# Unread matrix products by bank and by need, a norm's root on VectorE, and new charges in the planner of a four-layer hybrid kernel

## The chip, the cores and the metric

The kernel runs on one core of a Trainium2 chip. The metric is the device time of one launch in microseconds (us). In the notation of the profile, PE is TensorE's matrix products, PEld its weight loads, DVE is VectorE, ACT is ScalarE, POOL is GpSimd and SP is SyncE, which here only issues transfers.

## The reference

A token matrix `x` of 512 x 1024 goes through four layers. Each adds a mixer of the normalised activations and then a gated feed-forward block; a last norm ends it. The four mixers are different: a recurrent one with a state per head (RWKV-7), a banded attention, a chunked gating unit, and gated linear attention. Everything is float32.

```python
def rwkv7_mix(x, ...):
    ...
    def step(state, inp):
        r_t, d_t, k_t, v_t, kk_t, a_t = inp
        sa = jnp.einsum('bhvk,bhk->bhv', state, kk_t)
        state = (state * d_t[:, :, None, :]
                 - sa[..., None] * (kk_t * a_t)[:, :, None, :]
                 + v_t[..., None] * k_t[:, :, None, :])
        return state, jnp.einsum('bhvk,bhk->bhv', state, r_t)
    ...
    mean = jnp.mean(y, -1, keepdims=True)
    var = jnp.mean(jnp.square(y - mean), -1, keepdims=True)
    y = ((y - mean) * lax.rsqrt(var + RW_GN_EPS)).reshape(B, S, D) * gn_g + gn_b
    ...

def reference(x, ...):
    h = x
    for i in range(DEPTH):
        hn = rmsnorm(h, norm_mix[i])
        m = rwkv7_mix(hn, ...) if i == 0 else swa_sink_mix(hn, ...) if i == 1 else sgu_chunk_mix(hn, ...) if i == 2 else gla_mix(hn, ...)
        h = h + m
        h = h + swiglu(rmsnorm(h, norm_ffn[i]), ffn_w_in[i], ffn_w_out[i])
    return rmsnorm(h, norm_final)
```

The part that the change edits in the computation is the norm over each head's 64 values (`mean`, `var`, the reciprocal root) behind the recurrence; there are 16 heads.

## The kernel before, in words

**Products.** A float32 weight is split into a rounded part (`whi`, cast on ACT) and the rest (`wlo`, subtracted on DVE); the activations likewise. Each product is then three matrix products that accumulate in one bank of PSUM (`mm3`). The feed-forward blocks use a seven-product scheme for 2 x 2 blocks (`seven`, `hidden`, `out_fast`), whose sums DVE takes out of the banks into `slot` and `h`. PSUM has eight banks, one tile `ps` each.

**The recurrent mixer** fills the span up to about 520 us. The projections come first. Then four groups of four heads (`n` = 0 to 3) each go through a *preparation* (`rwkv_prepare`, `rwkv_products`, `rwkv_inverse`, `rwkv_direct`) that makes, for eight blocks of 64 tokens, small triangular matrices and their inverses, and through a *chain* (`rwkv_chain`) that carries the state from block to block. `rwkv_inverse` has a row of about thirty small DVE instructions (`et<-et`) that depend on each other, and then rounds of 64 x 64 products, with their results copied or masked by ACT and DVE (`mt`, `iv`). In the chain each step goes from PE (`ps<-vu,tok`) to DVE (`st<-ps,pend`) and back to PE. After every second pair of blocks `rwkv_out` takes the head norm, transposes on PE (`ps<-ident,out`) and splits the result (`rk`); it runs eight times in all. `rwkv_out_proj` multiplies the first six of eight pieces by the output weights while the last group's norm runs, and `out_proj` the last two.

**The order.** Nothing is issued as it is written. `Program.record` keeps every instruction with its dependences, and `Program.run` then sets the order on all engines by a simulated clock: an instruction's price is `price` (line 264), the earliest candidate within a window of 700 is issued, and PSUM banks are handed out by free slots. In the program's own order, preparation and chain alternate by `ORDER = "pppppcpcpcpc"` (line 31): five pieces of the next group's preparation, then chain and preparation by turns. Each engine executes its own row in the order that the planner left, so a wrong price costs a wait on the chip.

**Unread products.** The planner also issues products of the 128 x 128 identity with itself that nobody reads; line 478 (`product`) is their only source, and each takes a bank of its own. Two rules put them in. `keep_warm` (line 397) fills a gap on PE that the planner foresees and that is at least 450 ns long, one product after the other until the next real product is due. `ahead_of_cold` (line 416) puts one ahead of a real product when the columns that went through PE in the last 3,413 ns would fall under `DENSE` = 3,550. A product is charged 224 ns, or 448 when the window before had under `BUSY` = 3,350 columns. A float32 product such as this one has two records in the trace.

**The head norm.** `rwkv_out` (line 1363) takes two sums on DVE. The mean, the variance and the root are small 128 x 8 instructions on POOL: the multiplication by 1/64 with a tile of constants, the same and an addition for the variance, and in `rsqrt8` (line 1400) one DVE instruction for the first guess and then thirteen on POOL, three rounds of four. The other norms use `rsqrt`, whose ten instructions are all on DVE.

## Time and profile before

| | us |
|---|---|
| median of 3 runs (2602.77 to 2609.27) | 2609.03 |
| the profiled execution | 2608.54 |
| span in the profile | 2606.8 |
| PE busy | 2550.0 |
| DVE busy | 1796.5 |
| ACT busy | 1317.5 |
| POOL busy | 371.2 |

The mean granted clock of PE is 0.995. Between the span and the execution's time lie 1.7 us. A row of the busy-time view by windows gives a stretch, its length, and for each engine the busy time with the number of records in brackets, then the granted clock (1.00 is full), the share of the DMA engines and their rate. A row of the timeline gives the start, the length, the engine, the line, the operation, what it writes and reads, and the number of merged records; in square brackets stands the time that the engine sat idle before it, and what ended that. Nearly every instruction carries line 234, where the recorder calls the engine; so the names of tiles tell instructions apart, and line 478 the unread products. PE's ends are modelled: the distance between two starts is the better measure there.

### The profile page before, as it was taken

To read this page: it belongs to the slowest core of one execution; us is meant where nothing else is said; L and a number is where in the kernel's file an instruction comes from. 1 tells how busy PE (TensorE), PEld (TensorE's weight loads), DVE (VectorE), ACT (ScalarE), POOL (GpSimd) and SP (SyncE) were. 2 spreads that over 40 slices of the span, in tenths; PEclk is the share of its full clock that TensorE was granted. 3 is DMA by queue.
4 is the path that set the end of the run, shared out by engine and by line. 5 is a ranking of instruction groups with operands and counts; after the bars stand their busy time and mean duration, and the time that the engine had idled before them with its cause. 6 is when DMAs were issued, how large, how long until landed. Compare 5 with 4: busy or idle time off the path is not lost.

```text
span 2606.8 us, 37773 instructions
## 1 busy us (share of the span) xinstructions
PE 2550.0 (98%) x14482; PEld 2073.6 (80%) x14482; DVE 1796.5 (69%) x2801; ACT 1317.5 (51%) x2163; POOL 371.2 (14%) x517
## 2 busy tenths in 40 slices
PE   9999999999999999999999999999999999999998
PEld 8577777998878766988787888888878777888786
DVE  7674765478778864787777555477768634577868
ACT  4534354375646445655464333465546523555545
POOL 0000111112121332121212000012111000112111
PEclk9999999999999999999999999999999999999999
DMA  4210001379898422788995322399897221489885
GB/s 168 68 60 10 10 4 58 108 180 211 225 212 192 104 89 49 159 213 220 215 234 146 97 89 85 79 213 230 206 214 183 93 81 57 95 215 225 217 196 127
DMA packets 126581, 367.32 MB, mean 141 GB/s; under 512 B 13360, under 2 KB 20016, under 8 KB 126400
## 3 DMA queue, kind: packets, MB, share of 16 engines
q0 software_dynamic: 41472, 138.43, 29.7%
q1 hardware_dynamic: 84928, 226.47, 26.8%
q8 instruction: 114, 1.87, 0.3%
q14 instruction: 67, 0.55, 0.1%
HBM read 360.39 MB, written 2.10 MB: 139 GB/s over the span
## 4 chain that ended last, share of the span: by engine, by line
PE 50%; DMA 5%; DVE 4%; issue 3%; ACT 2%; POOL 0%; SPq 0%; DVEq 0%; POOLq 0%; ACTq 0%
PE ps L234 50%; DMA wraw<-ffn_w_b 3%; DMA wraw<-ffn_o_a 2%; DVE slot L234 2%; ACT slot L234 1%; ACT whi L234 1%; DVE wlo L234 1%; DMA wraw<-ffn_w_a 1%; DVE h L234 0%; PE ps L478 0%; DVE mx L234 0%; POOL wraw L234 0%; DMA slot<-slot 0%; POOL slot L234 0%; SPq L234 0%
## 5 line engine op out<-in xcount | busy, mean ns | idle before, releaser
L234 PE MATMUL ps<-whi,slot 128*128 128x512 f32 (+1 forms) x5072 | 1556.0, 384 | 18.6 <-DVE h L234 8.2
L234 PEld LDWEIGHTS ps<-whi,slot 128*128 128x128 f32 x5072 | 941.8, 188 | 200.9 <-issue 24.1
L234 DVE TENSOR_TENSOR wlo<-wraw,whi 128x1024 fp32r<-128x1024 f32 (+2 forms) x632 | 725.9, 1154 | 402.0 <-ACT whi L234 399.1
L234 ACT CAST whi<-wraw 128x1024 fp32r<-128x1024 f32 (+3 forms) x632 | 625.5, 993 | 725.3 <-PE ps L234 551.7
L234 PE MATMUL ps<-wlo,slot 128*128 128x512 f32 (+1 forms) x2536 | 967.6, 382 | 1.3 <-DVE wlo L234 1.3
L234 PEld LDWEIGHTS ps<-wlo,slot 128*128 128x128 f32 x2536 | 476.1, 188 | 85.7 <-DVE wlo L234 5.4
L234 PE MATMUL ps<-slot,whi 128*128 128x512 f32 (+2 forms) x864 | 274.6, 396 | 0.4 <-DVE slot L234 0.3
L234 DVE TENSOR_TENSOR slot<-ps,slot 128x512 f32<-128x512 f32 (+2 forms) x287 | 154.9, 566 | 74.6 <-PE ps L234 54.3
L234 PEld LDWEIGHTS ps<-slot,whi 128*128 128x128 f32 (+2 forms) x864 | 156.8, 184 | 48.9 <-DVE slot L234 6.9
L234 POOL DMA_DIRECT2D wraw<-ffn_w_a x128 | 109.4, 855 | 513.3 <-DVE wlo L234 395.5
L234 PE MATMUL ps<-slot,wlo 128*128 128x512 f32 (+2 forms) x432 | 169.5, 393 | 0.0
L234 POOL DMA_DIRECT2D wraw<-ffn_w_b x64 | 54.8, 861 | 767.7 <-DMA wraw<-ffn_w_b 517.2
L234 DVE TENSOR_TENSOR slot<-left,slot 128x512 fp32r<-128x512 f32 (+1 forms) x214 | 137.7, 662 | 34.9 <-ACT slot L234 29.4
L234 DVE TENSOR_TENSOR h<-h,ps 128x512 f32<-128x512 f32 x192 | 127.2, 683 | 30.5 <-PE ps L234 29.0
L234 ACT CAST slot<-left 128x512 fp32r<-128x512 f32 (+1 forms) x214 | 123.9, 599 | 32.8 <-PE ps L234 26.4
L234 ACT COPY slot<-ps 128x512 f32<-128x512 f32 (+1 forms) x138 | 75.9, 564 | 57.9 <-PE ps L234 54.2
L234 PEld LDWEIGHTS ps<-slot,wlo 128*128 128x128 f32 (+2 forms) x432 | 79.5, 184 | 20.3 <-issue 3.3
L234 POOL DMA_DIRECT2D wraw<-ffn_o_a x64 | 54.7, 854 | 277.7 <-DVE wlo L234 161.0
L234 PEld LDWEIGHTS ps<-ident,slot 128*128 128x128 f32 (+2 forms) x672 | 67.8, 139 | 30.5 <-issue 7.5
L234 PE MATMUL ps<-ident,slot 128*128 128x128 f32 (+2 forms) x672 | 87.4, 265 | 2.9 <-DVE slot L234 2.1
L478 PE MATMUL ps<-ident 128*128 128x128 f32 x488 | 80.9, 302 | 4.4 <-DVE slot L234 2.2
L234 ACT COPY left<-ps 128x512 f32<-128x512 f32 x100 | 50.5, 556 | 56.9 <-PE ps L234 56.9
(279 smaller groups left out, 2301.5 us busy)
## 6 DMA issues: line engine op xcount, KB each, us to landing
wraw<-ffn_w_a SPq DMA_DIRECT2D x128, 512.0 KB, 6.4
wraw<-ffn_w_a POOLq DMA_DIRECT2D x128, 512.0 KB, 6.1
wraw<-ffn_o_a SPq DMA_DIRECT2D x64, 512.0 KB, 5.0
wraw<-ffn_o_a POOLq DMA_DIRECT2D x64, 512.0 KB, 8.1
wraw<-ffn_w_b SPq DMA_DIRECT2D x64, 384.0 KB, 3.4
wraw<-ffn_w_b POOLq DMA_DIRECT2D x64, 384.0 KB, 6.0
wraw<-ffn_o_b SPq DMA_DIRECT2D x16, 512.0 KB, 4.3
wraw<-ffn_o_b POOLq DMA_DIRECT2D x16, 512.0 KB, 8.0
```

The source lines that it names most:

```text
L234: op = self.add(eng.name, lambda: getattr(eng.target, what)(*map(real, args), **{k: real(a) for k, a in kw.items()}), *self.price(eng.name ...
L478: self.nc.tensor.target.matmul(self.ps.tile_pool.tile([P, S], F32, name="ps")[:, :P], self.ident.real(), self.ident.real(), start=True, st ...
```

## The change

1. The unread products come in batches: `products(n)` takes one bank and puts `n` products into it, where each had taken its own. `ahead_of_cold` computes how many are needed (at most four) instead of one at a time.
2. They are put in by a smaller need: `BUSY` and `DENSE` fall to 3,000 columns; `keep_warm` stops, once a count has reached `DENSE`, when the past window has over `RICH` = 4,200 columns. A product is also charged for a change of shape (`TURN`, 92 ns).
3. The head norm's mean, variance and root go from POOL to DVE: one `tensor_scalar` each for the mean and the variance and the common `rsqrt`. `rsqrt8` and the constant tiles `k8` are gone.
4. Charges: a DVE instruction that writes a state tile `st` is charged 90 ns more, one on 32 partitions 270 ns more, and no small POOL instruction less than 150 ns.

`ORDER` stays. The order on every engine follows from the new numbers. Over the whole program the unread products go from 244 to 154; PE's other 12,128 products, and their operands, are the same.

```diff
-    TICK, BUSY, DENSE = 10240 / 3, 3350.0, 3550.0
+    TICK, BUSY, DENSE, RICH = 10240 / 3, 3000.0, 3000.0, 4200.0
...
-            return 63.0 + n * (0.52 if fast else 2.1 if what == "tensor_tensor_scan" else 1.05) + 61.0 * columns, 250.0
+            slow = 90.0 if views[0].buf.name.startswith("st") else 270.0 if views[0].shape[0] == 32 else 0.0
+            return slow + 63.0 + n * (0.52 if fast else 2.1 if what == "tensor_tensor_scan" else 1.05) + 61.0 * columns, 250.0
...
-        return 37.0 + n * (0.83 if len(views) < 3 else 2.8 if views[0].dims[-1][0] < 32 else 2.4), 250.0
+        return max(150.0, 37.0 + n * (0.83 if len(views) < 3 else 2.8 if views[0].dims[-1][0] < 32 else 2.4)), 250.0
...
         while True:
-            c = 224.0 if work.get(int(t // self.TICK) - 1, 0.0) >= self.BUSY else 448.0
-            if t + c > s - self.TAIL:
-                return now
-            call()
-            self.fills += 1
+            c = 224.0 + (self.TURN if self.form[:2] != (P, P) else 0.0)
+            if work.get(int(t // self.TICK) - 1, 0.0) < self.BUSY:
+                c *= 2
+            if t + c > s - self.TAIL or self.armed and self.past(s) > self.RICH:
+                break
+            n += 1
...
-        cost = 224.0 if work.get(int(t // self.TICK) - 1, 0.0) >= self.BUSY else 448.0
-        call()
-        self.fills += 1
...
+        n = min(4, math.ceil((self.DENSE - sum_) / 280.0))
+        for _ in range(n):
+            cost = 224.0 + (self.TURN if self.form[:2] != (P, P) else 0.0)
...
-        def product():
-            self.nc.tensor.target.matmul(self.ps.tile_pool.tile([P, S], F32, name="ps")[:, :P], self.ident.real(), self.ident.real(), start=True, stop=True)
-        self.nc.warm = self.ps, product, self.nc.ops[-1]
+        def products(n):
+            t, i = self.ps.tile_pool.tile([P, S], F32, name="ps")[:, :P], self.ident.real()
+            for _ in range(n):
+                self.nc.tensor.target.matmul(t, i, i, start=True, stop=True)
+        self.nc.warm = self.ps, products, self.nc.ops[-1]
...
-        nc.gpsimd.tensor_mul(mean, mean, self.k8['mean'])
+        nc.vector.tensor_scalar(mean, mean, 1.0 / 64, None, op0=ALU.mult)
...
-        nc.gpsimd.tensor_mul(var, var, self.k8['mean'])
-        nc.gpsimd.tensor_add(var, var, self.k8['eps'])
-        self.rsqrt8(rs, var)
+        nc.vector.tensor_scalar(var, var, 1.0 / 64, 64e-5, op0=ALU.mult, op1=ALU.add)
+        self.rsqrt(rs, var)
...
-    def rsqrt8(self, y, x):
-
-        nc = self.nc
-        t = self.sm.tile([P, 8], F32, name="rs8")
-        nc.vector.tensor_scalar(y.bitcast(I32), x.bitcast(I32), -0.5, float(0x5f3759df), op0=ALU.mult, op1=ALU.add)
-        nc.gpsimd.tensor_mul(x, x, self.k8['half'])
-        for _ in range(3):
-            nc.gpsimd.tensor_mul(t, y, y)
-            nc.gpsimd.tensor_mul(t, t, x)
-            nc.gpsimd.tensor_add(t, t, self.k8['one5'])
-            nc.gpsimd.tensor_mul(y, y, t)
```

The rows of the order below are shown without their numbers; line 478 before and line 496 now are the unread products, line 234 all else.

**TensorE in the third group's inverse** (`rwkv_inverse` with the chain's products among its rounds; `mt`, `iv` and `pa` are tiles of the inverse, `vu`, `st` and `v` of the chain). Before the change the order reads:

```order
L234 MATMUL ps<-mt,pa 64x64 x3
L478 MATMUL ps<-ident 128x128
L234 MATMUL ps<-mt,pa 64x64
L478 MATMUL ps<-ident 128x128
L234 MATMUL ps<-mt,pa 64x64 x12
L234 MATMUL ps<-iv,mt 64x64 x3
L234 MATMUL ps<-vu,pr 64x64 x2
L234 MATMUL ps<-ident,out 128x128
L478 MATMUL ps<-ident 128x128
L234 MATMUL ps<-mt 64x64 x7
L478 MATMUL ps<-ident 128x128
L234 MATMUL ps<-mt 64x64
```

With the change it reads:

```order
L234 MATMUL ps<-mt,pa 64x64 x16
L234 MATMUL ps<-vu,pr 64x64 x4
L234 MATMUL ps<-v_2013,pa 64x64
L234 MATMUL ps<-qk 128x128 x2
L234 MATMUL ps<-mt 64x64 x4
L496 MATMUL ps<-ident 128x128
L234 MATMUL ps<-mt 64x64 x12
L234 MATMUL ps<-et,sel 4x512
L234 MATMUL ps<-iv,mt 64x64 x16
```

The round of sixteen `mt,pa` products stood in three pieces with an unread product between them; it now stands whole, and the next round has one unread product in it.

**TensorE in the banded attention** (the 64-row products of queries with keys, `slot`). Before the change the order reads:

```order
L234 MATMUL ps<-slot 128x256 x8
L478 MATMUL ps<-ident 128x128 x7
L234 MATMUL ps<-slot 128x128
L478 MATMUL ps<-ident 128x128 x2
L234 MATMUL ps<-slot 128x128
L234 MATMUL ps<-slot 128x256 x10
```

With the change it reads:

```order
L234 MATMUL ps<-slot 128x128 x2
L234 MATMUL ps<-slot 128x256 x8
L496 MATMUL ps<-ident 128x128 x4
L234 MATMUL ps<-slot 128x128 x2
L234 MATMUL ps<-slot 128x256 x10
```

Nine unread products in nine banks became four in one, and the second break is gone. At the second place of this kind seven became six.

**VectorE at a head norm beside an inverse** (`gvar` is the variance, `grs` the root, `et<-et` the row of the inverse, `st` the chain's state). Before the change the order reads:

```order
L234 TENSOR_SCALAR grs_2578<-gvar 128x8
L234 STREAM_TRANSPOSE et<-et 128x512
L234 TENSOR_TENSOR st_1396<-ps,pend 64x2x64
L234 TENSOR_TENSOR et<-et 128x2
L234 TENSOR_TENSOR st_1396<-ps,pend 64x2x64
L234 TENSOR_REDUCE et<-et 128x2
L234 TENSOR_TENSOR et<-et 128x8
L234 TENSOR_REDUCE et<-et 128x2x2
```

With the change it reads:

```order
L234 TENSOR_SCALAR gvar<-gvar 128x8
L234 STREAM_TRANSPOSE et<-et 128x512
L234 TENSOR_SCALAR grs_2489<-gvar 128x8
L234 TENSOR_TENSOR et<-et 128x2
L234 TENSOR_TENSOR rs_t<-grs_2489 128x8
L234 TENSOR_REDUCE et<-et 128x2
L234 SCALAR_TENSOR_TENSOR rs_t<-gvar,rs_t 128x8
L234 TENSOR_TENSOR et<-et 128x8
L234 SCALAR_TENSOR_TENSOR grs_2489<-rs_t,grs_2489 128x8
L234 TENSOR_REDUCE et<-et 128x2x2
```

The root's instructions now stand between those of the inverse, by turns, and the state's update, which stood ahead of the second of them, comes after the root.

More of the change, by code (lines that the diff above doesn't have):

```diff
@@ L433, in ahead_of_cold, with past @@
             return False
[L434 to L440 removed]
+        n = min(4, math.ceil((self.DENSE - sum_) / 280.0))
+        for _ in range(n):
+            cost = 224.0 + (self.TURN if self.form[:2] != (P, P) else 0.0)
+            if work.get(int(t // self.TICK) - 1, 0.0) < self.BUSY:
+                cost *= 2
+            self.form = P, P, 0
+            self.count(work, self.TICK, t, cost, 512.0)
+            t += cost
+        call(n)
+        self.fills += n
+        now["PE"] = t
+        return True
+    def past(self, end):
+        sum_ = 0.0
+        for b, e, c in reversed(self.recent):
+            if e <= end - self.TICK:
+                break
+            sum_ += c * (e - max(b, end - self.TICK)) / (e - b)
+        return sum_
     def count(self, work, span, t, cost, columns):
```

19 lines of the change are left out of this document (6 added, 13 removed).

## The prediction

> **What bounds the kernel now.** I read the page first, then the busy time by stretches for the whole core and for line 478 alone, then who waits for whom, then the timeline at single places. On the page:
>
> ```profile
> PE 2550.0 (98%) x14482; PEld 2073.6 (80%) x14482; DVE 1796.5 (69%) x2801; ACT 1317.5 (51%) x2163; POOL 371.2 (14%) x517
> L478 PE MATMUL ps<-ident 128*128 128x128 f32 x488 | 80.9, 302 | 4.4 <-DVE slot L234 2.2
> ```
>
> PE is busy for 98% of the span, and 488 of its records are the 244 unread products. They are 80.9 us by the profile, so what matters is where they lie, and whether PE would otherwise wait there. By stretches, the whole core in the first three rows (PE, PEld, DVE, ACT, POOL) and line 478 alone in the others (PE, PEld):
>
> ```profile
> 190.00:270.00 80.00, 78.08 (x918) 59.95 (x913) 39.39 (x81) 37.25 (x73) 6.82 (x22) 1.00 0.03 8
> 270.00:290.00 20.00, 18.35 (x212) 16.92 (x211) 19.01 (x39) 10.30 (x20) 8.27 (x21) 1.00 0.06 15
> 290.00:450.00 160.00, 154.27 (x2250) 123.59 (x2250) 106.04 (x222) 67.19 (x146) 23.09 (x72) 0.99 0.08 27
> ...
> 0.00:20.00 20.00, 17.80 (x134) 17.61 (x134) 1.00 0.90 315
> 190.00:270.00 80.00, 6.26 (x30) 4.17 (x30) 1.00 0.03 8
> 270.00:290.00 20.00, 11.27 (x98) 11.10 (x98) 1.00 0.06 15
> 290.00:450.00 160.00, 21.48 (x96) 13.82 (x96) 0.99 0.08 27
> 505.00:520.00 15.00, 5.46 (x46) 5.37 (x46) 1.00 0.60 121
> 900.00:1000.00 100.00, 8.77 (x32) 6.52 (x32) 0.93 0.24 74
> 520.00:900.00 380.00, 2.29 (x12) 2.23 (x12) 1.00 0.80 190
> 1000.00:2600.00 1600.00, 5.96 (x32) 5.80 (x32) 1.00 0.66 159
> ```
>
> Two records are a product: 67 stand in the start, 15 and 48 in the recurrent mixer outside 270 to 290 us, 49 within these 20 us, 23 in the mixer's tail, 16 in the attention, and 22 in all that follows, four more elsewhere. In the mixer PE is full and DVE and ACT are not, except from 270 to 290 us, where DVE is busy for 19.01 of 20 us. All that PE waits for between 190 and 450 us is this:
>
> ```profile
> PE ps L234 <- DVE mt L234: 2.6, 4, 1.1
> PE ps L234 <- DVE st L234: 2.6, 3, 1.2
> PE ps L234 <- DVE out L234: 1.7, 2, 1.2
> PE ps L234 <- DVE et L234: 0.7, 1, 0.7
> PE ps L234 <- ACT vu L234: 0.5, 3, 0.2
> PE ps L234 <- ACT et L234: 0.2, 1, 0.2
> ```
>
> That is 8.3 us of 260. So the mixer is bound by PE's own row, and what leaves this row there can shorten the time. The start, the tail and the 270 us stretch are bound by what the products cover.
>
> **The change part by part.** *Unread products in the mixer.* By the order, 63 of them outside the DVE stretch become 21. One of them costs more than its own time:
>
> ```profile
> 446.18 0.49 PE L478 MATMUL ps<-ident 128*128 128x128 f32 x2
> 446.60 0.32 PE L234 MATMUL ps<-iv,mt 64*64 64x64 f32 x2
> ```
>
> From the start of the unread product to the next real one pass 0.42 us. The two rows of the stretches give 27.74 us (6.26 and 21.48) for 63, 0.44 us each, so 42 fewer are 18.5 us of PE's row. At most all of it reaches the end, since PE is nearly never the one that waits; at least none, if DVE, ACT and the chain follow no faster. I take two thirds, 12 us, because the waits of 8.3 us are nearer to none than to the 18.5 us that would have to appear.
>
> *Unread products at the VectorE stretch.* 49 become 38 (8, 25, 4 and 1 in the new order). Here they are cover: PE waits for a norm.
>
> ```profile
> 277.31 0.20 POOL L234 TENSOR_TENSOR gvar<-gvar,k8mean 128x8 f32<-128x8 f32 x1 [4.16 <-DVE gvar L234]
> ...
> 283.33 1.08 DVE L234 TENSOR_TENSOR out<-out,grs 128x512 f32<-128x512 f32 x1 [0.68 <-POOL grs L234]
> ...
> 284.56 0.63 PE L234 MATMUL ps<-ident,out 128*128 128x128 f32 x4 [0.52 <-DVE out L234]
> ```
>
> POOL takes from 277.31 to 283.33, 6 us, for a variance and a root, and PE's next real product needs them. Fewer products alone gain nothing here; an earlier root can gain between 0 and these 6 us. The new order still foresees a gap of 38 products; eleven fewer of the stretch's 0.23 us (11.27 us over 49) are 2.5 us, which I take.
>
> *Unread products in the attention.* Nine and seven become four and six, each lot in one bank.
>
> ```profile
> 912.99 3.72 PE L478 MATMUL ps<-ident 128*128 128x128 f32 x14 [1.32 <-DVE slot L234]
> 916.64 0.79 PE L234 MATMUL ps<-slot 64*128 64x128 f32 x2
> 917.36 1.22 PE L478 MATMUL ps<-ident 128*128 128x128 f32 x4
> 918.51 0.80 PE L234 MATMUL ps<-slot 64*128 64x128 f32 x2
> ...
> 913.53 0.30 PEld L478 LDWEIGHTS ps<-ident 128*128 128x128 f32 x2 [0.25 <-PE ps L478]
> ...
> 975.12 4.17 PE L478 MATMUL ps<-ident 128*128 128x128 f32 x14 [0.92 <-DVE slot L234]
> ```
>
> The real products behind them show no wait of their own at 916.64 and 918.51, so the unread ones held them back. An unread product takes 0.52 us here (3.65 us over seven), because each waits for the bank that the one before has just left: 0.25 us at 913.53. In one bank that wait has no cause. Nine products hold PE for 3.65 + 1.15 = 4.8 us; four, at 0.23 to 0.55 us, for 0.9 to 2.2. Seven hold it for 4.1 us; six for 1.4 to 3.3. The gain is 3.4 to 6.6 us if the products behind are ready, 0 if they are not; I take 4.
>
> *Unread products in the feed-forward blocks* all go, 22 with their neighbours. This I cost at nothing, because each stands where PE waits anyway:
>
> ```profile
> 690.55 0.47 PE L234 MATMUL ps<-whi,slot 128*128 128x512 f32 x1 [0.16 <-DVE slot L234]
> 744.46 0.47 PE L234 MATMUL ps<-whi,slot 128*128 128x512 f32 x1 [2.52 <-DVE h L234]
> ...
> 2475.68 0.47 PE L234 MATMUL ps<-whi,slot 128*128 128x512 f32 x1 [2.00 <-DVE h L234]
> ```
>
> These are the first real products after an unread one, and each has waited for DVE as well. Four of them, one in each layer's block and the first and the last of them shown, wait 2 us and more for DVE to take a sum out of the bank (`h`). What goes is cover for the clock. Windows of the clock's grid, PE alone:
>
> ```profile
> 375.13:378.54 3.41, 2.56 (x26) 1.00 0.02 5
> 378.54:381.95 3.41, 3.02 (x9) 0.50 0.00 0
> 740.40:743.80 3.40, 1.54 (x8) 1.00 0.98 271
> 743.80:747.20 3.40, 2.74 (x12) 1.00 0.75 245
> ```
>
> The first window had PE busy for 75% and was followed by 3.41 us at half clock; the window of 740.40 had 45% and was followed by none. So it is not idle time that decides, but what goes through PE, and of the eight records at 740.40 two are the unread product's. Without them such a window may be followed by a half one, at 3.41/2 = 1.7 us. With the four places that is 0 to 6.8 us; I take one, 1.7. The Trainium skill says otherwise (TensorE: Matmul & The Clock Gate, the section on why this matters for your kernels): the clock falls with idle gaps of over about 3 us between bursts. By that rule, no gap here is long enough, the removed products were never needed, and the sum would be 1.7 us lower; the window of 375.13 speaks against it.
>
> *Start and tail.* 67 become 57 and 23 become 18, and six stand newly among the output products ahead of the tail. The start waits for data in any case: nothing. In the tail 5.46 us over 23 are 0.24 each: 1.2 us less, 1.4 more, so nothing either.
>
> *The norm's root.* Eight norms lose 16 POOL instructions each and bring DVE eleven (two for mean and variance, nine more of the root), 88 in all. DVE already runs this root on columns as small:
>
> ```profile
> 12.40 0.16 DVE L234 TENSOR_TENSOR rs_t<-rcol 128x4 f32<-128x4 f32 x1
> 12.60 0.16 DVE L234 SCALAR_TENSOR_TENSOR rs_t<-ms,rs_t 128x4 f32<-128x4 f32 x1
> ...
>   POOL grs L234: 3.3, 5
> ```
>
> From start to start it is 0.20 us, so DVE gets 17.6 us more, and loses 3.3 us of waiting for POOL's `grs`. Queued behind the eleven are the inverse's row and the state's update, for which the chain on PE waits. DVE idles for 40.6 of 80 and 54 of 160 us on either side of the full stretch, which hides most. In that stretch a norm and a half are on the path, 16 instructions or 3 us. I take 3, with -3 (the waits gone, all else hidden) and 17.6 as ends.
>
> *Charges.* They have no price of their own; they act through the order, where rounds of sixteen products that stood in pieces now stand whole.
>
> The sum: -12 - 2.5 - 4 + 1.7 + 3 = -13.8 us. Against the profiled execution's 2608.54 us that is 2594.7, say 2595 us. The profiled execution lies 0.5 us under the median of 2609.03, which changes nothing; the gain on the median is 0.5%.
>
> **The rivals.** A measurement of this kernel can tell about 0.3% from no change, 7.8 us: faster is under 2601.2, slower over 2616.9.
>
> *All of PE's row comes out* (0.22). The 18.5 us arrive whole, the root's 6 us and the attention's 6.6 too, and DVE hides the new instructions: 2608.5 - 31.1 = 2577. For it speaks that PE waits only 8.3 us in 260; against it, that every shortening puts DVE and ACT nearer.
>
> *The waits take the place* (0.19). The 18.5 us come back as waits for `mt`, `st` and `vu`, since the chain is one dependence after another. Then -2.5 - 4 + 1.7 + 3: 2606.7, no change. In its favour are the chain's rounds through DVE and ACT; against it DVE's idle time, which is spent waiting for PE.
>
> *The clock falls in the mixer* (0.04). Where products between small real ones go, a window may be followed by one at half clock, as 375.13 was, at 1.7 us each. One of the 76 windows between 190 and 450 us was followed so before; seven more eat the 12 us, again 2606.7. Against it speaks that the mixer's row also gets denser as the products go. The Trainium skill has a rule that points there (TensorE: Matmul & The Clock Gate, part 4 on PE-mode transposes): transposes do not count as PE's work for the clock, so the mixer's many transposes would leave only the unread products to hold it. No row here tells transposes apart.
>
> *VectorE's row becomes the bound* (0.15). In the mixer the root's eleven instructions stand between the inverse's and ahead of the state's update (the third place of the order). If DVE is full where they fall, as from 270 to 290 us, each delays inverse and chain, PE's saving is a wait, and the whole 17.6 us show: 2608.5 + 17.6 - 3.3 - 4 + 1.7 = 2620.5 us. It decides from the point where DVE's share in 290 to 450 us goes from 106 of 160 us to near 19 of 20. I put the rest of what could make it slower, an unlucky order above all, into this chance.
>
> That the change does less than it says is not open: the order has 154 products in 30 rows, and no POOL instruction of the root.
>
> **How the numbers follow.** The forecast has 0.40 (2590 to 2601), the whole row 0.22, the waits 0.19, the clock 0.04, DVE 0.15. So faster is 0.62, no change 0.23, slower 0.15. The range goes from 2577, the second case, to 2614: the third case with all four places of the clock, 2606.7 + 5.1, and the 2.5 us at the norm not come. What lies outside is most of the slower case and a little under the second.
>
> **What would show it.** Right, step by step: between 190 us and the start of the output products the stretch is some 12 us shorter, with about 59 unread products where 112 were, and PE's waits for `mt`, `st` and `out` grow from 8.3 us by less than 7; in the attention the two places hold PE for 1 to 3 us each; POOL has no `grs`, and DVE some 17 us more of 128 x 8 instructions; from 1000 to 2600 us the same time within 5 us. Wrong: PE's waits in the mixer of 20 us or more (the waits), DVE without idle time beside an inverse and `st` late (DVE), or more than five half-clock windows between 190 and 450 us, where there was one.

## The result and the profile after

The change makes the kernel faster: a median of 2572.25 us (four runs, 2568.02 to 2575.44) against 2608.68, a ratio of 0.9864 with a 95% interval of 0.9843 to 0.9886, or 36 us. The forecast of 2595 us has the side right and the size wrong; 2572 lies under its range. The profiled execution after took 2575.44 us with a span of 2573.7, so the two profiles differ by 33.1 us.

Two rows of the profile after: PE's busy time on the page, and the unread products in the groups by form (count of records, then shortest, median and longest in ns, and when the first and the last start).

```profile
PE 2515.4 (98%) x14302; PEld 2047.2 (80%) x14302; DVE 1803.3 (70%) x2889; ACT 1312.9 (51%) x2161; POOL 338.4 (13%) x385
...
L496 PE MATMUL ps<-ident x308: 270/275/583, 1.4 to 948.9; 128*128 128x128 f32 x154
```

PE has 34.6 us less, and no unread product stands behind 949 us. To see where the time went, I compare the same products in both kernels, counted in the order in which the program records them: from the 900th to the 2,800th (the mixer behind its first projections) and from the 4,600th to the 5,000th (the attention). In these two stretches the busy time of the whole core, then of line 478 alone, before:

```profile
213.30:509.00 295.70, 285.98 (x3440) 236.01 (x3440) 183.77 (x385) 130.62 (x270) 44.83 (x144) 0.99 0.11 35
899.40:1023.30 123.90, 118.45 (x526) 76.75 (x525) 74.66 (x164) 65.19 (x212) 43.67 (x40) 0.94 0.25 70
213.30:509.00 295.70, 35.15 (x206) 26.63 (x207) 0.99 0.11 35
899.40:1023.30 123.90, 8.77 (x32) 6.52 (x32) 0.94 0.25 70
```

The same stretches after the change, the unread products being line 496:

```profile
214.10:491.20 277.10, 266.58 (x3355) 226.25 (x3356) 192.17 (x473) 126.64 (x268) 11.43 (x16) 0.98 0.11 37
878.70:992.70 114.00, 109.36 (x514) 69.90 (x513) 73.92 (x164) 64.91 (x212) 43.60 (x40) 1.00 0.26 77
214.10:491.20 277.10, 18.82 (x124) 15.65 (x125) 0.98 0.11 37
878.70:992.70 114.00, 3.03 (x20) 2.46 (x20) 1.00 0.26 77
```

The mixer's stretch is 18.6 us shorter and the attention's 9.9; the start is 0.8 longer, the 390 us between the two 2.9 shorter, what follows 2.5 shorter. Together 33.1. A stretch's length splits into four: unread products (the row of their line), PE idle (length less PE's busy time), time lost to the clock (half the length of its half-clock windows), and the other products (the rest of PE's busy time).

| us | unread | PE idle | lost to the clock | other products | length |
|---|---|---|---|---|---|
| mixer before | 35.2 | 9.7 | 1.7 | 249.1 | 295.7 |
| mixer after | 18.8 | 10.5 | 5.1 | 242.7 | 277.1 |
| attention before | 8.8 | 5.4 | 6.8 | 102.9 | 123.9 |
| attention after | 3.0 | 4.6 | 0 | 106.3 | 114.0 |

In the mixer the unread products give 16.3 us, and PE's idle time grows by only 0.8. The real products, which are the same, take 6.4 us less: that comes with their new order. (The split is rough where much runs at half clock: a run below that holds this order comes to 240.2 us of other products by it, 2.4 less.) In the attention more than half, 6.8 of 9.9 us, is the clock. Before, these two stretches ran at half clock there (the figure behind the five engines is the granted clock):

```profile
914.43:921.26 6.83, 6.77 (x31) 5.51 (x31) 3.59 (x7) 0.00 (x0) 0.00 (x0) 0.50 0.99 360
975.87:982.70 6.83, 6.71 (x30) 5.55 (x31) 4.17 (x10) 0.00 (x0) 0.00 (x0) 0.50 0.21 58
```

After the change none does. (The 3.5 us by which its other products grow are partly the split: at half clock PE also waits less, so half the length is more than what is lost.)

Who PE waits for in the mixer after the change, from 190 to 432 us (engine, tile, us in total, times, longest), the five largest rows:

```profile
PE ps L234 <- DVE mt L234: 3.2, 5, 1.4
PE ps L234 <- ACT vu L234: 1.6, 4, 1.0
PE ps L234 <- DVE et L234: 1.0, 2, 0.8
PE ps L234 <- ACT ew L234: 0.9, 1, 0.9
PE ps L234 <- DVE st L234: 0.6, 1, 0.6
```

With six smaller rows they are 9.5 us of 242, where 8.3 of 260 stood before; waits did not take the products' place. The two places in the attention, on PE's timeline:

```profile
891.65 1.16 PE L496 MATMUL ps<-ident 128*128 128x128 f32 x8 [0.67 <-DVE slot L234]
892.74 3.19 PE L234 MATMUL ps<-slot 64*128 64x128 f32 x24
...
947.28 1.93 PE L496 MATMUL ps<-ident 128*128 128x128 f32 x12 [0.67 <-DVE slot L234]
949.14 2.21 PE L234 MATMUL ps<-slot 64*128 64x128 f32 x19
```

Four products hold PE for 1.09 us and six for 1.86, 0.27 and 0.31 us each where one took 0.52. The clock did fall elsewhere. Three windows after the change (PE's and the other engines' busy time, the granted clock behind them):

```profile
248.67:252.08 3.41, 2.62 (x17) 1.76 (x16) 3.34 (x7) 0.00 (x0) 0.00 (x0) 1.00 0.26 82
252.08:262.32 10.24, 10.24 (x58) 8.05 (x57) 6.50 (x14) 1.20 (x2) 0.00 (x0) 0.50 0.00 0
1866.58:1870.00 3.42, 3.42 (x10) 2.65 (x9) 1.03 (x1) 0.49 (x1) 0.00 (x0) 0.50 0.63 190
```

Behind a window in which PE was busy for 77% come 10.24 us at half clock. The one at 1866.58 is in a feed-forward block, as the prediction had allowed for once. The Trainium skill (TensorE: Matmul & The Clock Gate, the section on why this matters for your kernels) ties such falls to idle gaps of over about 3 us; the window ahead of 252.08 has 0.79 us of idle time in all, so the trace disagrees again.

### The profile page after: what moved, and what is told of

The parts are those of the page before. It is cut to its first block, busy times and chain, and to the rows that moved or that the text cites. A ratio compares the mean times of both kernels' runs of the same rounds, so it can differ in the third digit from the quotient of the medians.

```text
span 2573.7 us, 37359 instructions
## 1 busy us (share of the span) xinstructions
PE 2515.4 (98%) x14302; PEld 2047.2 (80%) x14302; DVE 1803.3 (70%) x2889; ACT 1312.9 (51%) x2161; POOL 338.4 (13%) x385
## 4 chain that ended last, share of the span: by engine, by line
PE 52%; DVE 5%; DMA 3%; ACT 3%; issue 2%; POOL 0%; SPq 0%; DVEq 0%; ACTq 0%; POOLq 0%
PE ps L234 52%; DVE slot L234 2%; DMA wraw<-ffn_w_b 2%; ACT slot L234 2%; DVE wlo L234 1%; ACT whi L234 1%; DMA wraw<-ffn_o_a 1%; DVE mx L234 1%; DVE h L234 0%; DVE left L234 0%; ACT left L234 0%; DMA slot<-slot 0%; SPq L234 0%; POOL wraw L234 0%; DVE rs_t L234 0%
## 5 line engine op out<-in xcount | busy, mean ns | idle before, releaser
L234 DVE TENSOR_TENSOR slot<-left,slot 128x512 fp32r<-128x512 f32 (+1 forms) x214 | 138.3, 664 | 34.6 <-ACT slot L234 29.1
L234 DVE TENSOR_TENSOR slot<-slot 128x512 fp32r<-128x512 f32 (+9 forms) x93 | 61.2, 664 | 16.9 <-ACT slot L234 14.6
```

The lines of the kernel that those rows point to most:

```text
L234: op = self.add(eng.name, lambda: getattr(eng.target, what)(*map(real, args), **{k: real(a) for k, a in kw.items()}), *self.price(eng.name ...
```

## The experiments

Theories: **products** (the gain is unread products leaving PE's row), **norm** (VectorE makes the head norm shorter), **charges**, and **order** (what counts is the order that the planner makes, with its shapes and its half-clock stretches, whatever the edit meant to do). The times in us are the ratio to before times 2609.

**Two thirds of the mixer's products, order held.** The planner counts them, but 42 of 63 are not issued.

```diff
+            if 71 <= (n := self.nc.fills) < 86 and n % 3 or 135 <= n < 183 and n % 3:
+                return
```

> The kernel before, its order on every engine unchanged, but two of every three of the 63 unread products in the mixer outside the 270 us stretch are left out when they would be issued (42 fewer, as many as the change takes out there; the order was planned with them). Theory of PE's row: each takes its 0.44 us out of the end, 42 x 0.44 = 18.5 us, so 2590 us against 2608.7 of before. The prediction's reading (two thirds): -12, 2597. Theory of the order (the time of the change comes from a new order, not from products): waits for DVE and ACT take the place, -6 to 0. If the clock falls instead, half-clock windows appear between 190 and 450 us at 1.7 us each.

Measured: 2595.66 us, ratio 0.9948 (0.9934 to 0.9963), -13.6 us. The mixer's stretch, whole and line 480 alone:

```profile
212.30:497.60 285.30, 270.12 (x3366) 224.18 (x3367) 183.58 (x385) 130.61 (x270) 44.79 (x144) 0.99 0.11 36
212.30:497.60 285.30, 20.06 (x134) 16.45 (x134) 0.99 0.11 36
```

The unread products fall by 15.1 us, PE's idle time rises from 9.7 to 15.2, and the stretch is 10.4 shorter: two thirds come out, as forecast. The changed kernel took out about as much (16.3) with 0.8 more idle time, because its order was planned anew.

**One bank, order held.** An unread product that directly follows another uses its bank.

```diff
+            if p.bank is None:
+                p.bank = self.ps.tile_pool.tile([P, S], F32, name="ps")[:, :P]
+            p.tensor.target.matmul(p.bank, i, i, start=True, stop=True)
```

> The kernel before, its order unchanged, but unread products that directly follow each other share one bank. Nothing else is taken out. The prediction's reading: an unread product in the attention costs 0.52 us because of the bank and 0.3 without, so 16 x 0.22 = 3.5 us less, 2605 us. Theory that the attention's half-clock windows (914 and 976 us, 6.8 us each) came from the slow row of unread products: they go too, another 3 to 7 us, 2598 to 2602. Theory that the products behind them were not ready: no change, 2608.7.

Measured: 2603.4 us, ratio 0.9975 (0.9965 to 0.9985), -6.5 us. In its profile the attention has one half-clock window of 3.4 us where before had 13.7, so the gain is more than the 3.5 us of the products alone. The price of the bank and that of the clock can be told apart at the second place, which runs at full clock here:

```profile
972.50 1.83 PE L483 MATMUL ps<-ident 128*128 128x128 f32 x14 [1.18 <-DVE slot L234]
974.26 3.19 PE L234 MATMUL ps<-slot 64*128 64x128 f32 x24
```

Seven products in one bank take 1.76 us, 0.25 each. In the kernel before, the first three at 912.99 us took 0.55 each in banks of their own, also at full clock. So the bank's price was real; the four behind them, at half clock, took 0.50.

**Parts alone and in pairs.** Each is the kernel before with some parts of the diff.

> The kernel before with the first two parts alone: unread products by bank and by need, the norm on POOL and the old charges. 171 products where before has 244 and after 154. Theory of the products: nearly the whole gain, -30 us or more, 2572 to 2579. Theory that the parts add up with the charges' order as an equal share: -15 to -22, 2587 to 2594. The prediction's reading for these two parts: -12 - 2.5 - 4 + 1.7 = -16.8, 2592.

Measured: 2593.64 us, ratio 0.9936 (0.9918 to 0.9953), -16.7 us. The sum of the prediction for these parts was -16.8. That it met so well is partly luck: by place the mixer's stretch gave 7.1 and the attention 6.5, where 14.5 and 4 were forecast. In the mixer the unread products fell by 12.1 us and the other products by 4.3, but PE's idle time grew by 5.9 and the clock took 3.4 more.

> The kernel before with the fourth part alone: the new charges, unread products by the old rules, the norm on POOL. The planner then foresees more waits and puts in 313 products where before has 244: 103 where 63 stood in the mixer outside the 270 us stretch, and 48 where 16 stood in the attention. Theory of the products: 40 x 0.44 = 17.6 us more in the mixer and up to 32 x 0.52 = 16.6 us more in the attention, 2615 to 2643 us, slower. Theory of the order: the charges' order in the mixer gives 10 to 20 us, which meets these costs: 2595 to 2625. The prediction's reading: the charges have no price of their own, so only the products count.

Measured: 2633.03 us, ratio 1.0096 (1.0080 to 1.0112), +25 us. With the old rules the charges make the planner foresee more gaps and fill them. Of the 22.5 us by which its profile is longer only 2.4 are in the mixer's stretch; 18.8 lie behind it, where the attention has 3.4, 13.7 and 10.2 us at half clock.

> The kernel before with the third part alone: the head norm's mean, variance and root on VectorE, products and charges as before. The products' parts alone gave -16.7 us of the change's -36.4, as the prediction had them, so some 20 us are open. Theory of the norm (the 6 us that POOL takes for a root at 277 us and the waits for it at the other seven norms were on the path): -10 to -20, 2590 to 2600. The prediction's reading: +3, 2613, with 17.6 more at most. Theory of the charges: 0 to +3, as the gain lies in the order that the charges make once products are put in by need.

Measured: 2593.25 us, ratio 0.9934 (0.9915 to 0.9953), -17 us (-15.6 by the medians, as later expectations have it). This is the term that failed: +3 was forecast. By place, the mixer's stretch gave 8.2 of the profile's 18.1 us, the attention 6.0, all else 3.9.

> The changed kernel with the charges of before (parts one to three). Theory of the norm: nearly all of the change, -33 to -36, 2573 to 2577. Theory of the charges: as the products alone or a little slower, -14 to -17, 2593 to 2596. If the norm and the charges share the rest: about -26, 2584.

Measured: 2578.32 us, ratio 0.9885 (0.9869 to 0.9901), -30 us.

> The changed kernel with the norm's root on POOL as before (parts one, two and four; 184 unread products). Theory of the charges: -33 to -39, 2571 to 2577. Theory of the norm: -14 to -17, 2593 to 2596. If they share the rest: about 2584. Charges alone gave +24 with the old rules for products, which a mechanism that only works together with the rules by need has to explain.

Measured: 2597.31 us, ratio 0.9954 (0.9939 to 0.9970), -12 us. Its mixer's stretch is 6.1 us shorter than with the products alone (282.5 against 288.6), but from 951.06 us on its attention ran 30.7 us at half clock. So the charges made it slower by 25 alone and by 5 beside the products, and faster by 6 (36 against 30) beside products and norm: no price that could stand in a sum.

**The norm on VectorE, order held.** The planner still counts the sixteen instructions of each norm as POOL's and issues them at the same places, but they go to VectorE.

```diff
+        self.moved = Engine(self, "POOL", nc.vector)
...
-        nc.gpsimd.tensor_mul(var, var, self.k8['mean'])
+        nc.moved.tensor_mul(var, var, self.k8['mean'])
```

> The kernel before with its order held: the planner still counts the head norm's POOL instructions as POOL's, but they run on VectorE at the places where they were issued (16 at each of eight norms, 128 in all, where the change brings eleven). Unread products, their places and all else are those of before. Theory that VectorE itself shortens the norm: the 6 us of the root at 277 us become 16 x 0.2 = 3.2, and the 3.3 us of VectorE's waits for the root go: -3 to -8, 2601 to 2606. Theory of the order (the -15.6 of the third part alone came from the order that the planner made out of it, in the mixer and the attention): 0 to +5, 2609 to 2614. The prediction's upper end, a full VectorE row: 128 x 0.20 = 25.6 - 3.3, 2631.

Measured: 2617.71 us, ratio 1.0031 (1.0020 to 1.0043), +8 us. At one place the profile shows the queue that the prediction feared, on DVE's timeline:

```profile
263.27 0.17 DVE L235 TENSOR_SCALAR grs<-gvar 128x8 int32<-128x8 int32 x1
263.55 0.17 DVE L235 TENSOR_TENSOR gvar<-gvar,k8half 128x8 f32<-128x8 f32 x1
263.63 0.70 DVE L235 STREAM_TRANSPOSE et<-et 128x512 f32<-128x512 f32 x1
264.26 0.13 DVE L235 TENSOR_TENSOR rs<-grs 128x8 f32<-128x8 f32 x1
264.42 0.17 DVE L235 TENSOR_TENSOR rs<-rs,gvar 128x8 f32<-128x8 f32 x1
264.50 0.28 DVE L235 TENSOR_TENSOR st<-ps,pend 64x128 f32<-64x128 f32 x1
```

Behind the root's instructions stands the state's update `st`. PE's product on it, and two windows of the clock's grid:

```profile
265.39 0.82 PE L235 MATMUL ps<-st,ident 128*128 128x128 f32 x4 [1.55 <-DVE st L235]
...
265.80:282.87 17.07, 17.07 (x59) 10.63 (x59) 11.81 (x38) 8.43 (x15) 2.70 (x4) 0.50 0.02 7
262.39:265.80 3.41, 1.86 (x9) 0.90 (x8) 3.16 (x17) 1.13 (x3) 0.00 (x0) 1.00 0.00 0
```

In the kernel before the same product waits less:

```profile
263.36 0.68 PE L234 MATMUL ps<-st,ident 128*128 128x128 f32 x4 [0.63 <-DVE st L234]
```

With 0.92 us more of waiting PE is busy for 1.86 of 3.41 us, where the kernel before has 2.78 at this place, and 17.07 us at half clock follow: 8.5 of the 10.3 us by which the mixer's stretch is longer here. That the wait set the clock off is read from this one place. Over the nine runs the time goes from 2610.88 to 2622.59 us and the mean granted clock from 0.993 down to 0.989, so the half clock is not the same in each. Without it the mixer has 2.2 us more idle time (11.9 against 9.7). So in this order the engine alone costs about what the prediction took, 3, and gains nothing.

**The norm back on POOL, the new order held.** The counterpart: each instruction that the planner counts as VectorE's is executed as one or two on POOL.

```diff
+        self.moved = Engine(self, "DVE", Root(self, nc))
...
+        if a == -0.5:
+            g.tensor_mul(o, t, x)
```

> The changed kernel with its order held, but the head norm's mean, variance and root run on POOL at the places where the order has them for VectorE (the first guess stays on VectorE). The counterpart of the run that put them on VectorE in the order of before, which was slower by 8 us, 8.5 of them a half-clock stretch, and otherwise by about 1. Theory that the engine itself matters little and the order all: within 4 us of 2572. Theory that VectorE's shorter root is the gain: a 6 us root at the stretch and the other seven in part, +6 to +16, 2578 to 2588.

Measured: 2580.5 us, ratio to before 0.9886 (0.9866 to 0.9906), 8 us slower than the change by the medians. The mixer's stretch and one window of it:

```profile
210.50:497.60 287.10, 273.00 (x3355) 232.08 (x3356) 182.73 (x385) 127.34 (x268) 44.81 (x144) 0.95 0.11 35
...
375.20:388.87 13.67, 12.88 (x100) 10.73 (x101) 9.49 (x17) 3.43 (x8) 1.11 (x2) 0.50 0.03 11
```

It is 10 us longer: 3.6 more idle time, and 27.3 us at half clock instead of 10.2, which is 8.5 us. The time lies in the second theory's range, though most of it is the clock and not the root's own length. Ahead of the window shown, DVE waits for POOL's root, PE waits for DVE, and PE is busy for 1.60 of 3.41 us:

```profile
374.75 1.08 DVE L262 TENSOR_TENSOR out<-out,grs 128x512 f32<-128x512 f32 x1 [2.36 <-POOL grs L214]
375.99 0.45 PE L262 MATMUL ps<-ident,out 128*128 128x128 f32 x1 [2.59 <-DVE out L262]
```

In the changed kernel DVE waits for no root. So the two orders that were held disagree on what the engine is worth: VectorE costs 8 us in the order made for POOL and saves 8 in the order made for VectorE, and each time the larger part is the clock. And with the norm on POOL the new order, with its fewer products, still keeps 30 of the 36 us.

**The order as a control.** The planner's window of candidates is 680 instead of 700; nothing else is changed. First the kernel before, then the changed one.

```diff
-    WINDOW, SLACK, SEM = 700, 200.0, 100.0
+    WINDOW, SLACK, SEM = 680, 200.0, 100.0
```

> A control for the order: the kernel before, only the planner's window of candidates is 680 instead of 700. Everything computed is the same; 225 unread products where 244 stand, 56 in the mixer outside the norm's stretch where 63 stand, 15 in the attention where 16 stand. Theory that the order's luck is small: within 4 us of 2608.7, of which 7 x 0.44 x 0.73 = 2 us are the products. Theory that any new order of this planner moves the time by as much as the open part of the change: 10 us or more to either side.

Measured: 2611.84 us, ratio 1.0008 (0.9998 to 1.0019), +2 us. By place it differs more: the mixer's stretch is 4.5 us longer (300.2), the attention 1.8 shorter (122.1). In the mixer PE's unread and other products take 3.2 and 4.1 us less than before, but 17.1 us run at half clock (before 3.4), of which 10.2 begin behind these waits for POOL's root:

```profile
288.15 1.08 DVE L234 TENSOR_TENSOR out<-out,grs 128x512 f32<-128x512 f32 x1 [1.77 <-POOL grs L234]
289.38 0.30 PE L234 MATMUL ps<-ident,out 128*128 128x128 f32 x1 [1.84 <-DVE out L234]
```

> The same control for the changed kernel: the planner's window is 680 instead of 700. 160 unread products where 154 stand, 19 in the attention where 10 stand. Theory that the order's luck is small: within 4 us of 2572. Theory that it is large: 10 us or more to either side; the attention's 19 products, among the 64-row products again, should then make it 2580 us or more, as the changed kernel with the old norm (17 products there) lost 19 us on it between the attention's start and end.

Measured: 2577.87 us, ratio to before 0.9892 (0.9877 to 0.9908): 28 us faster than before, 6 slower than the change, between the two theories. Its mixer's stretch is 5.9 us shorter still (271.2), and its attention 12.5 longer, with this window:

```profile
952.51:966.16 13.65, 12.09 (x26) 4.89 (x25) 4.69 (x16) 8.27 (x31) 6.98 (x7) 0.50 0.00 0
```

The same kernel again:

> A second look at the changed kernel with a window of 680, for its attention: the first showed 13.7 us at half clock there and 19 unread products, and 9 us lost between the attention's products and its end. If the half clock comes from the order, it is there again; if from chance on the chip, not.

Measured: 2586.22 us in one run, and in the same place:

```profile
952.66:969.73 17.07, 15.29 (x38) 7.15 (x38) 7.02 (x20) 11.01 (x43) 10.11 (x12) 0.50 0.00 0
```

So the half clock at this place came again with the order, but how long it lasts differs from run to run, and the second run has another 6.8 us of it from 884.4 us on, where the first had none.

**Products and norm alone, with this window.**

> The first two parts alone (products by bank and by need), planned with a window of 680: 137 unread products where these parts had 171 at a window of 700, 225 where the kernel before has this window; 8 in the attention. Theory that products by bank and by need are worth 17 us or more in any order: 2580 to 2595, as 84 products fewer than in the control's mixer and attention count 0.44 us each at two thirds, 25 us at most. Theory that this gain too hangs on the order: 2600 or more.

Measured: 2585.08 us, ratio 0.9912 (0.9897 to 0.9928), -23 us, and 25 against the control with this window. The products' gain holds in another order.

> The third part alone (the norm on VectorE), planned with a window of 680: the pair to the control of the kernel before with that window (+2 us against before). 252 unread products where the norm alone had 230 at a window of 700: 28 in the attention where 11 stood. Theory that the norm on VectorE is worth its -17 us in any order: 2594 or less. Theory that the -17 was the order that fell out with it: 2600 to 2616, with the attention, at 28 products, losing the 6 us that it gained, or more.

Measured: 2605.79 us, ratio 0.9985 (0.9975 to 0.9995), -4 us, and 6 against the control. The stretches of the norm alone with the window of 700, mixer and attention, then line 478 in the attention:

```profile
213.20:500.70 287.50, 275.47 (x3422) 231.33 (x3422) 191.86 (x473) 125.40 (x266) 10.52 (x16) 1.00 0.12 37
889.90:1007.80 117.90, 113.80 (x515) 73.08 (x515) 74.20 (x164) 65.01 (x212) 43.60 (x40) 0.97 0.27 74
889.90:1007.80 117.90, 5.19 (x22) 3.45 (x22) 0.97 0.27 74
```

The same with the window of 680:

```profile
213.50:498.70 285.20, 276.89 (x3432) 231.85 (x3432) 190.33 (x473) 130.85 (x271) 9.91 (x16) 1.00 0.12 38
887.70:1019.10 131.40, 126.08 (x549) 82.81 (x549) 75.68 (x164) 66.04 (x212) 43.04 (x40) 0.92 0.23 66
887.70:1019.10 131.40, 15.01 (x56) 12.09 (x56) 0.92 0.23 66
```

The mixer's stretch is 8.2 and 10.5 us shorter than before's 295.7, in both orders and without a half-clock window. The attention, which has no head norm, is 6.0 shorter in one (11 unread products) and 7.5 longer in the other (28). Against its own control (300.2 and 122.1) the norm with the window of 680 has 15.0 us less in the mixer and 9.3 more in the attention. So the norm's -17 was a mixer's gain that came back in both orders, and an attention's gain that was the order's luck. The mixer's gain is not made of the same terms, though: with the window of 700 it is products (unread 4.0, others 4.8), with 680 the clock (8.5) and PE's idle time (6.3).

**The price of a change of shape.** 384 more unread products in the start, in blocks.

```diff
+                    for _ in range(48):
+                        mm(t[:64, :64], j, j, start=True, stop=True)
+                    for _ in range(48):
+                        mm(t, i, i, start=True, stop=True)
+                    for _ in range(48):
+                        mm(t[:64, :64], j, j, start=True, stop=True)
+                        mm(t, i, i, start=True, stop=True)
```

> A price by itself. The changed kernel with 384 more unread products of float32 in the start, twice the same three blocks in one bank: 48 of 64x64, 48 of 128x128, then 48 of each by turns. Its time as a whole says nothing; what counts is the length of the third block against the sum of the first two. Theory of the order (a change of shape on PE costs time): 95 changes make the third block longer, by 5 us or more of about 18 if a change costs what the mixer suggests (9.1 us of real products for 63 changes fewer, 0.14 us each, though other things may be in it). Theory that shapes cost nothing: the third block is as long as the first two together.

Measured, on PE's timeline: the block of 64x64, the block of 128x128, the first row of the third block, and the first behind it.

```profile
10.01 5.81 PE L501 MATMUL ps<-ident 64*64 64x64 f32 x96
15.75 10.98 PE L503 MATMUL ps<-ident 128*128 128x128 f32 x96
26.67 0.33 PE L505 MATMUL ps<-ident 64*64 64x64 f32 x2
...
58.99 0.38 PE L501 MATMUL ps<-ident 64*64 64x64 f32 x3
```

From start to start the blocks take 5.74, 10.92 and 32.32 us. By turns the same products take 15.7 us longer, some 0.165 us for each of about 95 changes. An unread 128x128 product between two 64x64 ones thus costs 0.23 of its own and two changes, 0.56 us.

**Fewer products in the new order.** First none behind the start, then none but the attention's ten.

```diff
+            if self.nc.fills >= 61:
+                return
```

> The changed kernel with its order unchanged, but none of the 93 unread products behind the start is issued: 21 in the mixer outside the norm's stretch, 38 in it, 24 at the output products and the tail, 10 in the attention. Theory of PE's row: 21 x 0.44 x 0.73 (the share that came out when 42 were left out of the kernel before) = 6.7 us less, and about 2 in the attention, 2563 us. Theory of the clock: where 38 and 18 in a row are missing, half-clock windows follow, and more of them between small real products: at 1.7 us each, 6 or more of them take it all back, 2573 us and over.

Measured: 2566.24 us, ratio to before 0.9833 (0.9815 to 0.9851), 6 us faster than the change.

> The changed kernel, its order unchanged, with no unread product behind the start but the 10 of the attention. With none at all it took 2566.2 us, with half-clock windows of 6.8 and 10.2 us in the attention where the changed kernel had none; from the attention's start to its end it lost 4 us on the changed kernel. Theory that the attention's products are worth their place: 2562 us. Theory that they cost what they save: 2566.

Measured: 2562.86 us, ratio to before 0.9825 (0.9812 to 0.9838), as expected: faster than both kernels, 46 us under before and 9 under the change. So most of what the change keeps is not needed either. One more step, the window of 680 with eight unread products in the attention and none else behind the start, brought less:

> A version that the runs point to: the changed kernel planned with a window of 680 (whose mixer was 9 us shorter than the changed kernel's in the profiles), with no unread product behind the start except eight in the attention. Theory that the gains add: the window's mixer -9 and the dropped products -9.4 (as dropping them gave from 2572.3 to 2562.9), less what the attention's order loses, up to 9: 2554 to 2563. If the clock falls in the attention as it did with this order: 2563 and over.

Measured: 2579.1 us, ratio to before 0.9876 (0.9854 to 0.9898). Its attention had 27.3 us at half clock; the gains did not add.

## Why the prediction was wrong, point by point

**The bound** was right: PE's row in the mixer, with waits that stayed at 9.5 us.

**The mixer's products** (-12 and -2.5 at the VectorE stretch) were sized right as what leaves PE's row: 16.3 us of unread products went. What of it reaches the end is not one share: two thirds with the order held, as argued; about half (7.1 of 14.5) with these parts alone and a new order; and in the whole change all but 0.8 us of idle time and 3.4 of the clock.

**The attention** (-4) was too small. The products gave 5.7 us there, near the 6.6 that was the upper end, and the clock 6.8, which the step had not looked at, although both half-clock stretches stood in the profile before, each beginning among the unread products that it priced. Nor is it a price: in other orders the attention lost them again.

**The norm's root** is the step that failed. It was costed by its instructions in the order as it stood, +3, beside -3 and 17.6 as ends. Alone it gave -17: 20 of the 22.6 us by which the gain was missed (36.4 against 13.8). In the order of before its direct price was near the forecast, 2.2 us of idle time. Even the 17.6 was too much: the 88 instructions add 8.4 us to DVE's busy time in the mixer's stretch (192.2 against 183.8), since by turns with others one can take less than 0.20: behind the one at 287.66 us in the changed kernel the next instruction starts after 0.08 us.

What the step had no term for is the order that the planner makes for the new engine, and the clock behind a wait. Four pairs differ by the norm and have an order planned for each: alone, alone with the window of 680, beside the products, and beside products and charges. The mixer's stretch is 8.2, 15.0, 4.8 and 5.4 us shorter with the norm on VectorE, the whole kernel 17, 6, 13 and 23 us faster. The terms change from pair to pair: alone the unread products took 4.0 us less, the other products 4.8, the clock 1.7, and PE's idle time grew by 2.3; in the other three pairs PE's idle time fell by 6.3, 5.9 and 3.2 us. One cause can be seen: where the order puts POOL's root on the path, `out` waits for it, PE for `out`, and 10.2 and 13.7 us at half clock followed in the two kernels shown above; on VectorE there is no such wait. In the order of before it was small (3.3 us of DVE's waiting), so it does not explain the -17 of the norm alone. That this order was better by products that no one edited, and that the attention gained 6.0 us with it, is the planner's luck as far as the runs show; why the planner found it stays open.

The root itself did not become the quick step that one would think. In the changed kernel it runs by turns with the inverse, and at this norm it takes 7.1 us from the first of these two rows to the end of the second, where POOL took 6:

```profile
285.86 0.16 DVE L234 TENSOR_SCALAR gvar<-gvar 128x8 f32<-128x8 f32 x1
...
292.84 0.16 DVE L234 SCALAR_TENSOR_TENSOR grs<-rs_t,grs 128x8 f32<-128x8 f32 x1
```

**The charges** ("no price of their own; they act through the order") were left out of the sum as nothing. They gave +25, +5 and -6 by what stood beside them.

**Feed-forward, start** (+1.7 and 0): 5.4 us less behind the mixer and outside the attention. The +1.7 came as forecast: at one of the four places, from 1863.16 us on, PE is busy for 1.39 of 3.42 us without its unread product, and 3.4 us at half clock follow. Why this part is shorter all the same is not traced. The reason given, that what goes through PE decides and not idle time, is not shown: PE busy for 41, 55, 75 and 77% of a window was followed by half clock and 45% was not, so busy time alone does not tell either.

So the working was sound for what leaves PE's row in a given order, and had no term for the order: 6.4 us of the mixer's other products and 6.8 of the attention's clock, of 33. Part of the 6.4 is changes of shape: leaving the unread products out, the size of the stationary operand changes 235 times from row to row of the stretch's trace before and 219 times after, 16 x 0.165 = 2.6 us. What the other 3.8 are stays open. Over the eleven orders on record, parts, pairs and controls, the changes go from 217 to 239 and the other products from 241.8 to 249.1 us, and they go together, at some 0.3 us a change, more than the price measured by itself. The order of before is one of the two with the most changes: the control with the window of 680, which computes the same, has 225 and 245.0 us. So a part of the 6.4 says that the order of before was a poor one, not that the change is good.

The rival that all of PE's row comes out named the right place and a time, 2577, that was near, though one of its three steps, the root's 6 us, is not what happened. And the range was too narrow: a control that computes the same moved the changed kernel by 6 us, and no bound stood for that.

## What to carry to other kernels

Where a planner sets the order, a part of a change has no price by its instructions alone: measure it once with the order held (the planner counts one thing, the chip executes another) and once planned anew, and run the same edit, and its control, with a planner number that should not matter. What falls out differently between the two is the order's luck, and a forecast's range has to hold it. An unread product that keeps the clock up must earn its own time and two changes of shape; drop them one lot at a time, since here the kernel was fastest with only ten of them behind the start.

## What the runs showed of the hardware

Where PE waited 0.92 us more, it was busy for 1.86 of 3.41 us, and 17.07 us at half clock followed, 8.5 us lost. A stretch at half clock lasted 3.4 to 17.1 us in these rows and 30.7 in the attention of products and charges; at the same place of the same kernel it lasted 13.65 us once and 17.07 the next time. Six unread products were enough to hold it off in the attention's second place. Without any, the changed kernel shows this there:

```profile
937.00:947.24 10.24, 9.11 (x31) 7.11 (x32) 10.21 (x26) 4.07 (x21) 0.00 (x0) 0.50 0.13 41
```

With the attention's ten, the same order shows no half clock in that place, though it still does for 6.8 us at the first one, which has four of them. And a change of shape between small float32 products costs PE some 0.165 us, more than a 64x64 product, which takes 0.12.
